# Third quarter of the up projection as seven half-size products, in a two-part encoder layer on one Trainium2 core

## The chip, the core and the metric

The kernel runs on one core of a Trainium2 chip. Five engines work beside each other, each through its own queue in order: TensorE (PE) multiplies, VectorE (DVE), ScalarE (ACT) and GpSimd (POOL) work on tiles, and SyncE (SP) issues nearly all transfers. The metric is the device time of one execution, in microseconds (us), as a median of runs.

## What is computed

One encoder layer for 512 tokens of width 1024 in float32. A token mixer (a bidirectional state-space scan and a windowed attention, merged by gates) is followed by an MLP. The change is in the MLP and in what feeds it; of the reference this matters:

```python
mixed = (g_ssd * y_ssd + g_attn * y_attn) @ w_o[l]
x = x + rmsnorm(mixed, post_mix_norm[l])
h = rmsnorm(x, pre_mlp_norm[l])
f = jnp.square(jax.nn.relu(h @ w_mlp_in[l])) @ w_mlp_out[l]   # 1024 -> 4096 -> 1024
x = x + rmsnorm(f, post_mlp_norm[l])
```

## The kernel before

**Three matmuls for one.** Each float32 operand is split into a high and a low part (`wh`, `wl` for weights, `th`, `tl` for weights split far ahead, `fh`, `fl` for activations). A product is three matmuls: high by high, high by low, low by high (`mm3`). ACT makes the high part (a cast, L1943 and L597). DVE or POOL subtracts to make the low part (L1946, and for plain weights L600 on DVE or L604 on POOL).

**Quarters.** The MLP is cut into four quarters of 1024 hidden columns. Each quarter has an up part (1024 to 1024, then squared ReLU) and a down part (1024 to 1024, summed over the quarters).

**Plain and folded.** A *plain* up product (`up_quantum`, `cm`) takes 128 hidden columns: 8 steps of 128 inputs, 3 matmuls each, so 24 matmuls of 128x512. Eight of them make a quarter: 192 matmuls. A *folded* quarter (`folded_quanta`) cuts both matrices into halves and uses seven half-size products in place of eight (Strassen's scheme in Winograd's form). Each of the seven has 2 token tiles, 4 steps and 3 matmuls, again 24 matmuls of 128x512, so a folded quarter takes 168. For that it needs sums of blocks. Of the weights: T3 = B22 - B12 (L1905), T2 = T3 + B11 (L1906), T1 = B22 - T2 (L1912), T4 = B21 - T2 (L1916), each in four tiles of 128x512. Of the activations: S1 to S4.

**What stands around a folded product.** A folded up quarter adds up its results in `up_summed` (an ACT copy at L1705 or a DVE sum at L1709), applies ReLU and square on ACT (L1712, L1714), writes halves of 16 bits apart (ACT, L1629) and stores them (`zt`). SP loads them back turned (L1638, DMA transposes). A plain product does ReLU and square on ACT (L1726, L1731) and stores `sd` (L1738). `combine` then makes the folded activations of a down quarter: on DVE four sums of 128x256 (L1784 to L1787) and four low parts (L540), on ACT four casts (L539), for each of four tiles. Down results are added into `acc` by DVE (L2049; the first into a tile is an ACT copy, L2046).

**Which quarters are folded.** `w_o`, up quarters 0 and 1 (`u0`, `u1`) and all four down quarters. Up quarters 2 and 3 are sixteen plain products. `build` lays them out by tables: two after `u1` (`LAG`), then by `STREAM` four among the products of down quarter 0, six among those of quarter 1, four among those of quarter 2, none in quarter 3.

**What sets the order.** The instructions are recorded in that order, and a `Planner` then fixes one order for each engine from costs and due times. On the chip every engine follows its list; a late operand holds up all that stands behind it. `SPL` gives three buffers each for `wh` and `wl`, so weights are split at most one and a half products ahead. Tables such as `LO_1` and `LO_2` say for each folded operand whether DVE makes the low part whole (`512`) or POOL in halves (`256`); `UPS_LO` says it for the plain products (`p` POOL, in three pieces, `d` DVE).

## Time and profile before

| | |
|---|---|
| median of 3 runs | 1026.97 us (1026.18 to 1027.3) |
| the profiled execution: its own time, its span | 1026.45 us, 1024.7 us |
| PE busy, of the span | 1016.6 us, 99% |
| DVE busy | 896.7 us, 88% |
| ACT busy | 721.1 us, 70% |
| POOL busy | 553.5 us, 54% |
| granted TensorE clock, mean | 0.999 |

Busy time overlaps between engines. Since matmuls are pipelined, the record of one (389 ns) is longer than the step from one to the next, so a run of matmuls is read by its length: 24 in 5.44 us. Stretches are given in us from the start of the span. `u0` and `u1` run from 723 to 778, down quarter 0 begins at 789, and the last matmul starts at 1017.5.

### The profile page before, as it was taken

What the parts mean: (1) busy time and instruction counts of PE and PEld (TensorE: products, weight loads), DVE (VectorE), ACT (ScalarE), POOL (GpSimd) and SP (SyncE); (2) the same over time, 40 slices, a digit from 0 to 9 for tenths busy, and PEclk for the clock granted to TensorE, in tenths of its full rate; (3) what the DMA queues carried; (4) which work ended last, traced back from release to release, by engine and by line L of the source; (5) the groups of instructions that cost most, each with busy time, mean ns of one, the idle gap of its engine ahead of it and who ended that gap; (6) DMA issues with size and microseconds to landing.
All of it is one profiled execution on the core that took longest, in us unless ns stands there. A gap on an engine that the chain in (4) does not pass through costs nothing.

```text
span 1024.7 us, 16500 instructions
## 1 busy us (share of the span) xinstructions
PE 1016.6 (99%) x5154; PEld 853.1 (83%) x5154; DVE 896.7 (88%) x1497; ACT 721.1 (70%) x1495; POOL 553.5 (54%) x571
## 2 busy tenths in 40 slices
PE   9999999999999999999999999999999999999997
PEld 8888888888888888888888888888888888888886
DVE  6886988879999899897999978789986999899997
ACT  7977959687797786968885324479999664555662
POOL 5967658476594866948898766222542223206001
PEclk9999999999999999999999999999999999999999
DMA  8389799998797999989976999875657785973482
GB/s 314 116 206 276 185 223 227 213 233 223 206 248 206 227 230 225 227 233 224 249 240 201 336 343 329 283 249 178 208 143 192 184 248 187 311 274 106 138 293 103
DMA packets 197976, 231.57 MB, mean 226 GB/s; under 512 B 102392, under 2 KB 120824, under 8 KB 197888
## 3 DMA queue, kind: packets, MB, share of 16 engines
q1 hardware_dynamic: 197600, 230.22, 79.1%
q8 instruction: 40, 0.66, 0.3%
q14 instruction: 48, 0.39, 0.1%
q10 hardware_dynamic: 288, 0.30, 0.1%
HBM read 161.97 MB, written 47.51 MB: 204 GB/s over the span
## 4 chain that ended last, share of the span: by engine, by line
PE 94%; DVE 3%; issue 1%; ACT 1%; POOL 0%; POOLq 0%; DVEq 0%
PE pp L522 58%; PE ps L522 35%; DVE wl L1946 1%; DVE tl L1946 1%; POOL wl L1946 0%; ACT wh L1943 0%; PE pp L526 0%; DVE wt L1912 0%; DVE wd L1906 0%; DVE pp L1709 0%; ACT acc L1705 0%; ACT th L1943 0%; DVE fs L1674 0%; DVE ps L1968 0%; ACT junk L2061 0%
## 5 line engine op out<-in xcount | busy, mean ns | idle before, releaser
L604 POOL TENSOR_TENSOR wl<-wr,wh 128x341 fp32r<-128x341 f32 (+1 forms) x330 | 346.2, 1064 | 267.3 <-ACT wh L597 259.6
L522 PE MATMUL pp<-h,wh 128*128 128x512 f32 x1376 | 426.3, 390 | 0.0
L522 PEld LDWEIGHTS pp<-h,wh 128*128 128x128 f32 x1376 | 256.2, 188 | 52.6 <-issue 0.7
L522 PE MATMUL pp<-h,wl 128*128 128x512 f32 x688 | 269.0, 391 | 0.0
L597 ACT CAST wh<-wr 128x1024 fp32r<-128x1024 f32 (+1 forms) x115 | 119.5, 1039 | 81.6 <-PE pp L522 48.9
L522 PEld LDWEIGHTS pp<-h,wl 128*128 128x128 f32 x688 | 129.1, 188 | 27.2 <-issue 0.5
L1943 ACT CAST wh<-wd 128x512 fp32r<-128x512 f32 x116 | 67.4, 619 | 39.6 <-PE ps L522 21.8
L1946 DVE TENSOR_TENSOR wl<-wd,wh 128x512 fp32r<-128x512 f32 x102 | 74.3, 758 | 6.6 <-ACT wh L1943 6.1
L522 PE MATMUL ps<-wl,fh 128*128 128x512 f32 x196 | 76.2, 390 | 0.3 <-POOL wl L1946 0.3
L522 PE MATMUL ps<-wh,fl 128*128 128x512 f32 x196 | 76.1, 389 | 0.0
L522 PE MATMUL ps<-wh,fh 128*128 128x512 f32 x196 | 75.4, 389 | 0.0
L1946 POOL TENSOR_TENSOR wl<-wd,wh 128x256 fp32r<-128x256 f32 x28 | 29.0, 1061 | 52.5 <-ACT wh L1943 20.9
L1326 ACT ACTIVATE n<-cb,tables 128x128 f32<-128x128 f32 x128 | 48.9, 392 | 9.3 <-DVE yT L1461 4.8
L1133 DVE SCALAR_TENSOR_TENSOR u<-pp,cv,u 128x510 f32<-128x510 f32 (+1 forms) x64 | 47.8, 747 | 6.4 <-ACT u L1129 4.2
L1946 DVE TENSOR_TENSOR tl<-wd,th 128x512 fp32r<-128x512 f32 x60 | 46.5, 799 | 5.1 <-ACT th L1943 5.0
L1327 ACT ACTIVATE m<-cb,tables 128x128 f32<-128x128 f32 x128 | 48.9, 390 | 0.0
L1322 ACT ACTIVATE rf<-rf,tables 128x128 f32<-128x128 f32 x128 | 42.1, 391 | 5.4 <-DMA rf<-csT 5.2
L522 PEld LDWEIGHTS ps<-wl,fh 128*128 128x128 f32 x196 | 36.8, 188 | 8.3 <-POOL wl L1946 0.7
L522 PEld LDWEIGHTS ps<-wh,fh 128*128 128x128 f32 x196 | 36.8, 188 | 7.7
L522 PEld LDWEIGHTS ps<-wh,fl 128*128 128x128 f32 x196 | 36.8, 188 | 7.5
L1008 DVE COPY dp<-P 128x768 uint16<-128x768 uint16 (+1 forms) x48 | 38.1, 809 | 4.6 <-ACT P L1038 3.7
L1320 POOL TENSOR_TENSOR rb<-rb,tables 128x512 f32<-128x512 f32 x32 | 39.9, 1251 | 2.7 <-DMA rb<-csT 2.6
(335 smaller groups left out, 2406.7 us busy)
## 6 DMA issues: line engine op xcount, KB each, us to landing
wr<-in_w_in_b SPq DMA_DIRECT2D x74, 512.0 KB, 5.3
wd<-in_w_mlp_out SPq DMA_DIRECT2D x76, 256.0 KB, 4.5
zt<-dp SPq DMA_DIRECT2D x56, 256.0 KB, 3.9
sd<-wd SPq DMA_DIRECT2D x48, 256.0 KB, 5.3
wd<-sd SPq DMA_DIRECT2D x48, 256.0 KB, 3.8
wd<-in_w_mlp_in SPq DMA_DIRECT2D x44, 256.0 KB, 4.9
rb<-csT SPq DMA_DIRECT2D x32, 256.0 KB, 4.6
rf<-csT SPq DMA_DIRECT2D x32, 256.0 KB, 6.1
```

The source lines that it names most:

```text
L522: self.nc.tensor.matmul(out, lhsT, rhs, start=start, stop=stop, skip_group_check=more)
L597: self.nc.scalar.copy(hi[:, :m], raw)
L604: self.nc.gpsimd.tensor_tensor(lo[:, c], raw[:, c], hi[:, c].bitcast(F32), op=ALU.subtract)
L1008: (copy or nc.vector.tensor_copy)(apart.rearrange("p (u k) -> p u k", u=2), src.bitcast(U16)[:, :2 * w].rearrange("p (k u) -> p u k", u=2))
L1133: nc.vector.scalar_tensor_tensor(u[:, a:e], ps[:, a + d:e + d], self.wtap(t, b), u[:, a:e], op0=ALU.mult, op1=ALU.add)
L1320: nc.gpsimd.tensor_tensor(v4(rb), v4(rb), cs[:, 1].unsqueeze(2).to_broadcast([128, 4, 128]), op=ALU.subtract)
L1322: nc.scalar.activation(v4(rf)[:, h], v4(rf)[:, h], AF.Identity, bias=ncs[:, 0, h:h + 1])
L1326: nc.scalar.activation(v4(n)[:, h], cb[:, 0], AF.Copy, scale=dt[:, 0, h:h + 1])
L1327: nc.scalar.activation(v4(m)[:, h], cb[:, 1], AF.Copy, scale=dt[:, 1, h:h + 1])
L1943: nc.scalar.copy(hi, src)
L1946: (nc.vector if q == 512 else nc.gpsimd).tensor_tensor(lo[:, c], src[:, c], hi[:, c].bitcast(F32), op=ALU.subtract)
```

## The change

It does these things.

- `FOLDED` is 3: the third up quarter becomes the folded `u2`. Its operands `S1` to `S4`, already made for `u0` and `u1`, are held one quarter longer. The low parts of its weights are all DVE's (`UP2_LO`).
- A string `SEQ` lays out the rest in place of `LAG`, `STREAM` and `NEXT_F`: seven products of `u2`, seven of down quarter 0, then the eight plain products that are left (`x`), six among those of down quarter 1 and two among those of quarter 2, then quarter 3. `F_AT` says when each `combine` is recorded.
- The low parts of the eight plain products are all DVE's (`UPS_LO`), in two instructions each.
- `ACCUM`: in down quarter 2, T1 and T4 are no longer DVE differences. ACT writes the negative of B11 (into a `wt` tile) and, when T2 has been split, of T2 (in place). A transfer from POOL's queue adds B12 or B21 from memory to it. That is 8 tiles.
- Smaller: halves of T1 and T4 in quarter 1 and of B22 in quarter 2 are POOL's, T2 and T3 of quarter 2 no longer. In the attention, 16 copies of 128x768 (L1008) go from DVE to ACT (`PARTED`). Scan groups 0 and 7 leave `SINGLE`, group 1 joins `JOINED`. Some lead times move by one or by a half. At the end two scalings go to ACT and POOL (`SHARED`). The planner gets costs for POOL's transfers.

In instructions (both lists counted): PE 24 matmuls of 128x512 fewer. DVE 26 low parts of folded weights (L1946), 8 weight sums (L1905, L1906), 6 sums of results (L1709) and 6 low parts of plain weights (L600) more, L1912 and L1916 the same in number. ACT 28 casts of folded weights, 8 negations, 6 copies (L1705), 8 copies of halves (L1629) more and 8 casts of plain weights fewer. POOL 33 pieces of L604 fewer, 4 halves and 8 transfers more. SP 16 transposes more.

```diff
-LO_1 = {'B11': [[(0, 256), (1, 256)], [(0, 512)]], 'B21': ...
-LO_2 = {... 'T2': [[(0, 256), (1, 256)], [(0, 512)]], ... 'T3': [[(0, 256), (1, 256)], [(0, 512)]], ...
+LO_1 = {... 'T1': [[(0, 512)], [(0, 256), (1, 256)]], ... 'T4': [[(0, 512)], [(0, 256), (1, 256)]]}
+LO_2 = {... 'B22': [[(0, 256), (1, 256)], [(0, 256), (1, 256)]], ...
-SINGLE = (0, 1, 2, 3, 4, 5, 6, 7)
+SINGLE = (1, 2, 3, 4, 5, 6)
-JOINED = (0, 3, 4, 5, 6, 7)
-FOLDED = 2
+JOINED = (0, 1, 3, 4, 5, 6, 7)
+FOLDED = 3
-SHARED = ((4, 3, 2),)
+SHARED = ((3, 2, 1), (4, 3, 1))
-PARTED = "DDD"
+PARTED = "DAD"
-UPS_LO = "pppppddppppddppdpdpp"
-STREAM = "0101011", "2110101", "2100100"
+SEQ = "uuuuuuu0000000x1x1xx111x1x12x2x22222"
+ACCUM = (2,)
+UPS_LO = "dddddddd"
...
+            if part in ACCUM and name == "T1":
+                return raw["T1", k], (("T1", k),)
+            if part in ACCUM and name == "T4":
+                return raw["B11", k], (("B11", k),) + ...
...
+                    if part in ACCUM and name in ("B11", "T2"):
+                        t = src
+                        if name == "B11":
+                            t = raw["T1", k] = get("wt")
+                        nc.scalar.activation(t, src, AF.Copy, scale=-1.0)
+                        nc.gpsimd.dma_start(t, block("B12" if name == "B11" else "B21", k), accum_op=ALU.add)
...
+        downs = {}
+        for d in SEQ + "3":
+            if d in "0123" and d not in downs:
                 for k in range(4):
-                    self.at(n() + FIRST_F[k], lambda k=k: self.up_combine(0, k))
...
+                    self.at(n() + F_AT[int(d)][k], lambda k=k, d=d: self.up_combine(int(d), k))
+                downs[d] = deque(self.folded_quanta(int(d)))
+            if d == "3":
+                self.add(*downs[d])
+            else:
+                self.add((more if d == "u" else ups if d == "x" else downs[d]).popleft())
```

On PE, at the end of `u1`, before the change (names end in buffer numbers; `h` are the normalised activations, `ps` and `pp` result banks):

```order
L522 MATMUL ps_8553<-th_9076,h_1038_8268 128x512
L522 MATMUL ps_8553<-tl_9077,h_1038_8268 128x512
L522 MATMUL ps_8553<-th_9076,h_1039_8269 128x512
L522 MATMUL pp_9230<-h_1024_8254,wh_9087 128x512
L522 MATMUL pp_9230<-h_1025_8255,wh_9087 128x512
L522 MATMUL pp_9230<-h_1024_8254,wl_9088 128x512
```

The same place after the change:

```order
L524 MATMUL ps_8559<-th_9082,h_1040_8274 128x512
L524 MATMUL ps_8559<-tl_9083,h_1040_8274 128x512
L524 MATMUL ps_8559<-th_9082,h_1041_8275 128x512
L524 MATMUL ps_9252<-wh_9095,h_1026_8260 128x512
L524 MATMUL ps_9252<-wl_9096,h_1026_8260 128x512
L524 MATMUL ps_9252<-wh_9095,h_1027_8261 128x512
```

The two plain products (first operand `h`, second `wh`) that stood between `u1` and down quarter 0 are gone from here; the first product of `u2` follows `u1` at once, and after seven such products quarter 0.

On DVE, from the last T4 sums of `u1` on, after the change (L1922 and L1923 are the sums that were L1905 and L1906, L1937 was L1916, L1967 was L1946):

```order
L1937 TENSOR_TENSOR wd_8100<-wd_8218,wd_8100 128x512
L1967 TENSOR_TENSOR tl_9070<-wd_8019,th_9069 128x512
L1967 TENSOR_TENSOR tl_9081<-wd_8098,th_9080 128x512
L1967 TENSOR_TENSOR wl_9096<-wd_9091,wh_9095 128x512
L1922 TENSOR_TENSOR wd_9193<-wd_9189,wd_9193 128x512
L1711 TENSOR_TENSOR acc_9045<-ps_8558,acc_9045 128x512
L1922 TENSOR_TENSOR wd_9195<-wd_9191,wd_9195 128x512
L1923 TENSOR_TENSOR wd_9091<-wd_9193,wd_9091 128x512
L1711 TENSOR_TENSOR acc_9059<-ps_8559,acc_9059 128x512
L1967 TENSOR_TENSOR wl_9184<-wd_9179,wh_9183 128x512
```

Low parts and sums of `u2` now fill DVE's list between the last sums of results of `u1`.

On POOL, the last part of the program, before:

```order
L604 TENSOR_TENSOR wl_10411<-wr_10400,wh_10410 128x342 x2
L604 TENSOR_TENSOR wl_10775<-wr_10723,wh_10774 128x341
L604 TENSOR_TENSOR wl_10775<-wr_10723,wh_10774 128x342 x2
L1946 TENSOR_TENSOR wl_10781<-wd_10633,wh_10780 128x256 x2
L1946 TENSOR_TENSOR wl_10824<-wd_10676,wh_10823 128x256 x2
L604 TENSOR_TENSOR wl_10864<-wr_10821,wh_10863 128x341
```

And after:

```order
L1967 TENSOR_TENSOR tl_9083<-wd_8100,th_9082 128x256 x2
L1967 TENSOR_TENSOR wl_10443<-wt_10448,wh_10442 128x256 x2
L1967 TENSOR_TENSOR wl_10508<-wt_10513,wh_10507 128x256 x2
L1967 TENSOR_TENSOR wl_10519<-wd_10050,wh_10518 128x256 x2
L1967 TENSOR_TENSOR wl_10558<-wd_10147,wh_10557 128x256 x2
L1973 DMA wt_10853<-in_w_mlp_out 128x512
L1973 DMA wt_10858<-in_w_mlp_out 128x512
L1973 DMA wt_10903<-in_w_mlp_out 128x512
L1973 DMA wt_10908<-in_w_mlp_out 128x512
L1973 DMA wd_10746<-in_w_mlp_out 128x512
L1973 DMA wd_10748<-in_w_mlp_out 128x512
```

POOL has nothing from the end of `u1` (`tl_9083`) to the halves of T1 of down quarter 1 (`wl_10443`), then two rows of T4 halves, then the transfers that add (six of the eight; two more follow the last row, and then the halves of B22 of quarter 2). The `L604` rows of before are gone.

## Rows read from the trace of the kernel before

**Rows 1.** The page: busy time by engine; the chain that ended last.

```profile
PE 1016.6 (99%) x5154; PEld 853.1 (83%) x5154; DVE 896.7 (88%) x1497; ACT 721.1 (70%) x1495; POOL 553.5 (54%) x571
PE 94%; DVE 3%; issue 1%; ACT 1%; POOL 0%; POOLq 0%; DVEq 0%
```

**Rows 2.** The waits of PE alone, 24 to 1018: total us, times, longest.

```profile
PE ps L522 <- POOL wl L1946: 0.3, 1, 0.3
```

**Rows 3.** The chain in order of time: start us, us, what.

```profile
757.72 3.11 POOL wl L1946
...
816.31 5.44 PE pp L522 x24
...
838.07 5.44 PE ps L522 x24
```

**Rows 4.** Busy us (instructions) by stretch: PE, PEld, DVE, ACT, POOL; clock, DMA share, GB/s.

```profile
720.00:760.00 40.00, 40.00 (x177) 32.91 (x176) 39.97 (x60) 37.99 (x68) 14.75 (x9) 1.00 0.55 168
760.00:778.00 18.00, 17.74 (x78) 14.36 (x78) 7.84 (x11) 17.13 (x27) 15.76 (x18) 1.00 0.70 192
778.00:854.00 76.00, 76.00 (x337) 62.90 (x336) 70.67 (x122) 53.98 (x95) 15.57 (x14) 1.00 0.76 212
854.00:940.00 86.00, 86.00 (x381) 71.22 (x380) 79.93 (x128) 44.37 (x77) 23.75 (x22) 1.00 0.69 232
940.00:1018.00 78.00, 77.74 (x355) 64.67 (x353) 71.18 (x127) 42.26 (x83) 6.97 (x8) 1.00 0.50 169
```

**Rows 5.** DVE in order of time: start us, us, instruction [idle before, releaser].

```profile
751.60 2.49 DVE L1912 TENSOR_TENSOR wt<-wd,wd 128x512 f32<-128x512 f32 x4
...
762.52 0.73 DVE L1946 TENSOR_TENSOR tl<-wd,th 128x512 fp32r<-128x512 f32 x1 [1.81 <-ACT th L1943]
...
768.29 0.70 DVE L1709 TENSOR_TENSOR pp<-pp,acc 128x512 f32<-128x512 f32 x1 [1.79 <-PE pp L522]
...
779.13 0.42 DVE L1784 TENSOR_TENSOR fs<-fT 128x256 f32<-128x256 f32 x1 [5.01 <-DMA fT<-zt]
```

**Rows 6.** Groups by shape, 670 to 1025: busy us, mean ns | idle before.

```profile
L1946 DVE TENSOR_TENSOR wl<-wd,wh 128x512 fp32r<-128x512 f32 x100 | 72.3, 754 | 6.0 <-ACT wh L1943 5.4
...
L1943 ACT CAST wh<-wd 128x512 fp32r<-128x512 f32 x113 | 65.6, 619 | 36.1 <-PE ps L522 19.1 <-PE pp L522 12.1 <-DVE wd L1916 2.5
...
L1629 ACT COPY dp<-r 128x1024 uint16<-128x1024 uint16 x16 | 16.7, 1044 | 0.3
...
L1916 DVE TENSOR_TENSOR wd<-wd,wd 128x512 f32<-128x512 f32 x16 | 12.9, 842 | 0.0
```

**Rows 7.** The line of the low parts: ns min/median/max, first and last start.

```profile
L1946 DVE TENSOR_TENSOR wl<-wd,wh x102: 676/686/1415, 649.6 to 999.8; 128x512 fp32r<-128x512 f32 x102
...
L1946 POOL TENSOR_TENSOR wl<-wd,wh x28: 735/924/3602, 649.6 to 944.2; 128x256 fp32r<-128x256 f32 x28
...
L1946 DVE TENSOR_TENSOR wl<-wt,wh x16: 680/688/693, 754.0 to 952.3; 128x512 fp32r<-128x512 f32 x16
```

**Rows 8.** POOL busy in L604 alone, by stretch.

```profile
778.00:1018.00 240.00, 32.24 (x28) 1.00 0.65 205
```

**Rows 9.** Transfers: count, KB each, median us to landing; the turned loads' issue ns.

```profile
wd<-in_w_mlp_out SPq DMA_DIRECT2D x76, 256.0 KB, 4.5
...
L1638 SPq DMA_TRANSPOSE fT<-zt x32: 1127/1246/1725, 754.4 to 834.4; - x32
```

**Rows 10.** A stretch of the scan: PE, PEld, DVE, ACT, POOL.

```profile
200.00:300.00 100.00, 100.00 (x609) 85.44 (x606) 89.11 (x158) 77.61 (x184) 67.45 (x72) 1.00 0.90 230
```

**Rows 11.** The last scalings, on DVE and on POOL.

```profile
1020.31 0.48 DVE L2080 SCALAR_TENSOR_TENSOR x<-ps,frs,x 128x256 f32<-128x256 f32 x1
...
1020.20 0.72 POOL L2077 TENSOR_TENSOR x<-x,sc 128x256 f32<-128x256 f32 x1 [0.58 <-ACT sc L2076]
```

More of the change, by code (lines that the diff above doesn't have):

```diff
@@ L41 @@
 MIX_FAR = (0,2,3,5,6,8,9,11,12)
-MIX_LEAD = (('B11', 5), ('B21', 4), ('B22', 3), ('B12', 3))
+MIX_LEAD = (('B11', 6), ('B21', 5), ('B22', 4), ('B12', 4))
 PP_BANKS = {("o", "Z"), (3, "Z"), ("u0", "Z"), ("u0", "Y"), ("u1", "Z"), ("u1", "Y")}
 PAIRS = (1, 0), (2, 3)
-SINGLE = (0, 1, 2, 3, 4, 5, 6, 7)
+SINGLE = (1, 2, 3, 4, 5, 6)
 NEXT_SCORES = False
-E_LEAD = 1
-JOINED = (0, 3, 4, 5, 6, 7)
+E_LEAD = 1.5
+JOINED = (0, 1, 3, 4, 5, 6, 7)
 ALONE = (7,)
-FOLDED = 2
+FOLDED = 3
 HALVES = 4 if FOLDED == 1 else 0
@@ L333, in duration @@
         if e == "POOL":
+            if "DMA" in kind:
+                return 1000, False
             if "pow" in str(getattr(i, "op", "")):
@@ L377, in deadlines @@
                 continue
-            c += LEAD if "DMA" in type(self.ins[n]).__name__.upper() else 0
+            c += 0 if "DMA" not in type(self.ins[n]).__name__.upper() else LEAD + SOFT + 1500 if e == "POOL" else LEAD
             late[n] = min([late[s] - self.AFTER[self.eng[s]] for s in self.post[n]] + [bound]) - c
@@ L421, in plan @@
             if e == "SP" or "DMA" in type(self.ins[n]).__name__:
-                queue = max(queue, t + ISSUE) + self.transfer(n, t)
-                free[e], end = end, queue + LAND
-                landed.append(end)
-                landed.popleft()
-                free["SP"] = max(free["SP"], min(landed) + 60)
+                soft = e == "POOL"
+                queue = max(queue, t + (ISSUE, 900)[soft]) + (1480 if soft else self.transfer(n, t))
+                free[e], end = end, queue + LAND + (0, SOFT)[soft]
+                if not soft:
+                    landed.append(end)
+                    landed.popleft()
+                    free["SP"] = max(free["SP"], min(landed) + 60)
             elif e == "PE":
@@ L1687, in flip_h2 @@
                                       "S3": [x[:, lo] for x in ft], "S4": [x[:, hi] for x in ft]}
-            self.held.setdefault(f"u{FOLDED - 1}", []).append({"S1": fs, "S3": ft})
+            self.held.setdefault(f"u{FOLDED - 1}", []).append({"S1": fs, "S3" if FOLDED < 3 else "S4": ft})
         if t2 == 0:
@@ L1885, in prepare @@
         def prepare(k):
+            if part in ACCUM:
+                a, b, c, d = (get("wd") for _ in range(4))
+                more = lambda t, src: nc.gpsimd.dma_start(t, src, accum_op=ALU.add)
+                nc.sync.dma_start(b, block("B12", k))
+                nc.sync.dma_start(c, block("B11", k))
+                nc.scalar.activation(b, b, AF.Copy, scale=-1.0)
+                more(b, block("B22", k))
+                more(c, b)
+                nc.scalar.activation(a, c, AF.Copy, scale=-1.0)
+                nc.scalar.activation(d, c, AF.Copy, scale=-1.0)
+                more(a, block("B22", k))
+                more(d, block("B21", k))
+                for t, n in ((c, "T2"), (b, "T3"), (a, "T1"), (d, "T4")):
+                    ready[n, k] = self.spill(t)
+                return
             a, b, c, d = (get("wd") for _ in range(4))
@@ L1909, in operand @@
                 return raw["B12", k], (("B12", k),)
+            if part in ACCUM and name == "T1":
+                return raw["T1", k], (("T1", k),)
+            if part in ACCUM and name == "T4":
+                return raw["B11", k], (("B11", k),) + ((("B21", k),) if order.index("A12") < order.index("A22") else ())
             if name == "T1":
@@ L2135, in build @@
         ups = deque(self.up_quantum(i) for i in range(8 * FOLDED + HALVES, 32))
[L2136 to L2156 removed]
+        downs = {}
+        for d in SEQ + "3":
+            if d in "0123" and d not in downs:
+                for k in range(4):
+                    self.at(n() + F_AT[int(d)][k], lambda k=k, d=d: self.up_combine(int(d), k))
[4 more added lines that the diff above has]
+                self.add((more if d == "u" else ups if d == "x" else downs[d]).popleft())
+        assert not more and not any(downs[d] for d in "012")
         assert not ups
```

36 lines of the change are left out of this document (7 added, 29 removed).

## The prediction

> **What bounds the kernel now.** I read the table of engines and the chain first. TensorE is busy for 1016.6 of 1024.7 us and holds 94% of the chain [rows 1]. Then the waits of PE alone: from 24 us to the last matmul there is one, of 0.3 us, on a low part that POOL makes [rows 2]; in the chain it is POOL's step at 757.72, and all else around it is PE with itself, 24 matmuls in 5.44 us or 226.7 ns each [rows 3]. The clock is 1.00 in every stretch [rows 4]. So the time falls by what PE has less to do, as long as no operand comes late. The stretches show who could be late. A row gives PE, PEld, DVE, ACT and POOL in this order: DVE is busy for 39.97 of 40 us at 720 to 760, then for 7.84 of 18, 70.67 of 76, 79.93 of 86 and 71.18 of 78; ACT is full only to 778, and from there has a quarter of its time free or more, POOL more than half [rows 4].
>
> **PE: the gain.** A plain quarter is 192 matmuls, a folded one 168, and the lists of PE for the whole program say the same: 4721 before, 4697 after. So the rival that the change doesn't take work off the bounding engine is out. At the price of rows 3 these 24 are **-5.44 us**, all on the path.
>
> **DVE: what is added, and its cover.** By the lists DVE gets from 760 on 26 low parts of folded weights, 8 weight sums, 6 sums of results and 6 low parts of plain weights more, and two scalings at the very end fewer: 44 instructions of 512 columns. A record lasts 680 to 690 ns undisturbed [rows 7], but records overlap: four L1912 take 2.49 us [rows 5], 0.62 each. 44 x 0.62 = **27.3 us**. PE also leaves 5.4 us less to do it in, so 32.7 us of idle time are wanted.
>
> The cover is DVE's idle time. From 760 to 778 it is 18 - 7.84 = 10.2 us, from 778 to 1018 it is 5.3 + 6.1 + 6.8 = 18.2 us [rows 4]: 28.4 us, 4.3 too few. A relief comes to it. POOL's pieces of plain weights, 28 of them with 32.24 us after 778 [rows 8], all go. Beside POOL a DVE instruction is slower: the same low part has a median of 688 ns from `wt`, where its spread is 680 to 693 [rows 7], and a mean of 754 from `wd` [rows 6]. The 66 ns over 100 such low parts are 6.6 us, without the sums, which are slowed too (L1916 has a mean of 842 ns, rows 6). How much of it goes with L604 is not to be seen; it lies between 0 and some 10 us, and I take **6 us**, near the one term that has rows. Then 32.7 stand against 34.4 us. The cover is just enough, with 1.7 us to spare in 250, and DVE is as full there as at 720 to 760.
>
> The Trainium skill ("SBUF — State Buffer", section "Who interferes with whom") says why such a relief should exist: a DVE instruction with two SBUF inputs contends with a GpSimd instruction that reads SBUF, since its second input comes through the shared read interface. The trace agrees: POOL's halves, 735 ns at best, reach 3602 ns [rows 7]. By the rule the relief could be as much as the whole 32 us of POOL reads that go, and the 1.05 us of the next paragraph would then be 0 and the sum 1022.0.
>
> Can a DVE that is full keep PE fed? Before, it was full from 720 to 760, and PE lost nothing till 757.7 and 18 - 17.74 = 0.26 us behind it [rows 4], so 0.26 us in some 58 us of that kind. After, the full stretch is some 235 us: 0.26 x 235 / 58 = **+1.05 us**. A part of the idle time looks hard to fill, since it ended on ACT's high part (1.81 us at 762.52), on a result of PE (1.79 us at 768.29) and on a turned load (5.01 us at 779.13) [rows 5]. But a DVE that has other rows in hand or is late itself doesn't wait for PE, and in its new list `u2`'s low parts and sums stand between the sums of `u1`'s results.
>
> **ACT.** 28 casts of folded weights and 8 negations at 0.62 us, 8 copies of halves at 1.04 [rows 6], 6 result copies (taken as casts) more, and 8 casts of plain weights at about 1 us fewer: some +26 us. After 778 ACT is idle for 22 + 42 + 36 us [rows 4], four times that. The tight place is the start: from 760 to 778 it is busy for 17.13 of 18, and its casts for `u2` begin there. A cast that is late passes its delay to DVE and from there to PE; this is in the range. **SP** gets 16 turned loads of 1.25 us at issue and 16 weight loads more and 8 stores and 16 loads fewer; the loads of 256 KB land in 4.5 us and the DMA share is 0.76 at most after 778 [rows 4, 9]. `u2`'s results are now loaded back among quarters 0 and 1 and used in quarter 2, some 100 us later. Nothing.
>
> **The scan and the tail.** There 16 copies go from DVE to ACT; in 200 to 300 DVE has 11 us free and ACT 22, and PE loses none [rows 10]. Nothing, as long as ACT takes 16 us over the whole of the scan. At the end DVE's last scaling begins at 1020.31 and POOL's at 1020.20 [rows 11]; one moved from DVE to ACT and POOL leaves the end where it is within 0.3 us.
>
> **The adding transfers.** No row shows one, or a POOL queue that issues one. From below, it is a load of 256 KB that lands in 4.5 us [rows 9], and it takes 8 sums of 0.62 us, 5 us, off DVE against the differences (which the count above has already, as L1912 and L1916 stay equal in number). From above, each issue holds POOL as long as its slowest half, 3.60 us [rows 7]. T4 is the tighter of the two: in PE's list T2's product is under way at row 4165, and T4's first matmul is row 4249, 84 x 0.2267 = 19.0 us. Negation 0.62, four issues 14.4, landing 4.5, cast 0.62, low part 0.69: 20.8 us, **1.8 us late** at the upper end, 0 at the lower. Only the two groups of four queue behind each other on POOL, then B22's halves. I am nearer to the lower end, since the half's median is 924 ns [rows 7], and take a quarter of it, **+0.45**.
>
> The Trainium skill warns of just this ("SBUF — State Buffer", section "SBUF: two separate sides"): a transfer issued from the GpSimd queue has its descriptors written by GpSimd's cores, and some DVE instructions lock these out. The page's other section, named above, infers that a tensor_tensor doesn't, since it takes the read interface alone. No row of before can show it; by the first the term would be 1.8 us and the sum 1024.4, by the second 0 and 1022.5.
>
> **The sum.** The profiled execution took 1026.45 us, 0.52 less than the median. 1026.45 - 5.44 + 1.05 + 0.45 = 1022.5; with the 0.52, **1023.0 us**.
>
> **The rivals.**
>
> *DVE takes PE's place as the bound.* If the relief is 0, DVE lacks 4.3 us. If, besides, a quarter of the 18.2 us that it was idle after 778 can't be filled, it lacks 4.5 us more. PE then waits for low parts all through `u2` and quarters 0 and 1, 8.8 us in all: 1026.97 - 5.44 + 8.8 = **1030.3 us**, slower than before. It decides from a loss of 5.44 + 2.1 = 7.5 us on. For it speaks the 70.67 of 76 us; against it that PE did not stand still beside a DVE that was wholly full. The place to fear is `u2` with quarter 0 behind it and no plain product between: some 54 rows of 0.62 us for `u2` and 44 us for quarter 0 are 77.5 us, in 76.2 us of PE's 336 matmuls. It has to live on the 10 us of before 778.
>
> *DVE is partly late.* Half of that, 4.4 us: 1026.97 - 5.44 + 4.4 = **1025.9 us**, the same as before within the bound.
>
> *The transfers are late.* T1 or T4 at the upper end, once or twice 1.8 us besides the 1.05: 1026.97 - 5.44 + 1.05 + 1.8 = **1024.4**, or up to 1026.2.
>
> *Full gain.* No loss at all: 1026.97 - 5.44 = 1021.5; the neighbour of the forecast, within its case.
>
> **How the numbers follow.** A measurement of this kernel tells some 0.2%, 2.05 us, from no change: faster is below 1024.9, slower above 1029.0. The forecast (1021.2 to 1024.4) has 0.58; DVE partly late (1024.4 to 1028) 0.18; late transfers 0.07; DVE as the bound 0.12; 0.05 is left for what I don't see, of either sign. Faster: 0.58, 0.06 of the late transfers, and 0.03 each from the edge of partly late and from the rest, about 0.68, taken as 0.67. Slower: 0.12 starts at about 1028, so two thirds of it: 0.08. Same: 0.25. The range goes from 1021.2 (the full gain and the spread of the runs) to 1026.8, where the case of partly late has been taken in to its greater part; some 0.15 lies above it and 0.03 below.
>
> **What would show it.** Right: PE's records 24 fewer in the up part, its waits after 24 us no more than 2 us in all, DVE busy for 97% or more from 770 to 940, POOL's halves nearer to 735 ns. If DVE is the bound, PE's waits stand at low parts of `u2` and quarter 0, released by L1946, with DVE at 100% ahead of them. If ACT is late, DVE's idle time ends on L1943. If transfers are late, the wait stands at T4 or T1 of quarter 2, released by a DMA. What makes the prediction wrong first is the relief: DVE's low part from `wd` staying at 754 ns beside a POOL that has little to do.

## The result and the profile after

The changed kernel takes 1030.11 us (median of 7 runs, 1029.56 to 1030.7), the kernel before beside it 1026.70 us (7 runs, 1026.18 to 1027.3). The ratio is 1.0034, with a 95% interval of 1.0022 to 1.0045: **3.4 us slower**, where the prediction said 3.9 us faster. It lies outside the range.

The profiled execution of after spans 1028.1 us, 3.4 us more than the one of before. The page's table of engines, and its chain, to hold against [rows 1]:

```profile
PE 1014.6 (99%) x5130; PEld 847.9 (82%) x5130; DVE 902.8 (88%) x1527; ACT 753.7 (73%) x1555; POOL 524.9 (51%) x552
PE 86%; DVE 4%; DMA 3%; ACT 3%; issue 1%; SPq 1%; POOL 1%; DVEq 0%; ACTq 0%; POOLq 0%
```

PE has its 24 matmuls fewer (5154 to 5130), so the 5.44 us were saved. But it holds 86% of the chain, no longer 94%: other engines and transfers now stand on it. PE's waits from 750 us on, where before had the one of [rows 2]:

```profile
PE ps L524 <- ACT fh L541: 2.1, 2, 1.3
PE ps L524 <- DVE wl L1967: 1.2, 2, 0.7
PE ps L524 <- POOL wl L1967: 1.2, 2, 1.0
PE ps L524 <- ACT acc L2073: 0.4, 1, 0.4
```

And the stretches, to hold against [rows 4] (PE, PEld, DVE, ACT, POOL; clock, DMA share, GB/s):

```profile
760.00:778.00 18.00, 16.83 (x74) 13.28 (x73) 11.29 (x17) 14.41 (x24) 12.89 (x12) 1.00 0.53 172
778.00:854.00 76.00, 75.07 (x328) 60.83 (x327) 73.03 (x130) 71.34 (x127) 0.00 (x0) 1.00 0.64 175
854.00:940.00 86.00, 85.31 (x377) 70.22 (x376) 81.20 (x141) 44.25 (x76) 13.34 (x12) 1.00 0.87 245
940.00:970.00 30.00, 27.80 (x120) 21.94 (x119) 29.58 (x57) 22.50 (x43) 6.09 (x7) 1.00 0.94 282
```

PE stands still in four places: at 764, 824 to 828, 932, and 943 to 949. ACT is as full as DVE from 778 to 854 (71.34 of 76 us; 53.98 before). From 854 on the transfers are: a DMA share of 0.87 and 0.94, where before had 0.69 and, at 940 to 970, 0.29.

**Where the time went.** To compare executions I add up, over successive matmuls, the time from start to start beyond what a matmul of that width takes without a wait (226.7 ns for 512 columns by [rows 3], and 0.42 ns less for each column fewer: steps of 320 columns have a median of 147 ns in the trace of before; less than 30 ns is left out). This is PE's *loss*, in us. It is a little more than the waits, since the step after a wait is some 0.1 us longer too, and in the scan it holds many short steps above that price, which both kernels have.

| | 0 to 24 | 24 to 600 | 600 to 755 | 755 to 778 | 778 to 850 | 850 to end |
|---|---|---|---|---|---|---|
| before | 4.3 | 27.0 | 1.8 | 0.5 | 0.0 | 0.0 |
| after | 4.7 | 28.2 | 1.8 | 1.7 | 1.9 | 4.0 |

The differences are 0.4, 1.2, 0, 1.2, 1.9 and 4.0: 8.7 us. With the gain, -5.44 + 8.7 = +3.3 us, which is the 3.4 us measured. So the question is what makes the losses of 1.9 us (at 824 to 828) and 4.0 us (at 930 to 949), and who is to blame for the rest.

### The profile page after: what moved, and what is told of

Read it like the earlier page. It is cut to its first block, busy times and chain, and to the rows that moved or that the text cites. A ratio compares the mean times of both kernels' runs of the same rounds, so it can differ in the third digit from the quotient of the medians.

```text
span 1028.1 us, 16576 instructions
## 1 busy us (share of the span) xinstructions
PE 1014.6 (99%) x5130; PEld 847.9 (82%) x5130; DVE 902.8 (88%) x1527; ACT 753.7 (73%) x1555; POOL 524.9 (51%) x552
## 4 chain that ended last, share of the span: by engine, by line
PE 86%; DVE 4%; DMA 3%; ACT 3%; issue 1%; SPq 1%; POOL 1%; DVEq 0%; ACTq 0%; POOLq 0%
PE pp L524 48%; PE ps L524 38%; DMA rb<-csT 1%; DMA E<-csE 1%; DVE u L1135 1%; DMA wd<-in_w_mlp_out 1%; DMA xt<-in_xt 0%; SPq L1885 0%; DVE w L1405 0%; DVE m L1331 0%; SPq L1306 0%; PE pp L528 0%; ACT rf L1324 0%; DVE ps L1400 0%; DVE C L1135 0%
## 5 line engine op out<-in xcount | busy, mean ns | idle before, releaser
L524 PE MATMUL pp<-h,wh 128*128 128x512 f32 x1248 | 386.8, 391 | 0.0
L606 POOL TENSOR_TENSOR wl<-wr,wh 128x342 fp32r<-128x342 f32 (+3 forms) x297 | 305.7, 1043 | 128.2 <-ACT wh L599 121.0
L524 PEld LDWEIGHTS pp<-h,wh 128*128 128x128 f32 x1248 | 232.1, 188 | 47.9 <-issue 1.0
L524 PE MATMUL pp<-h,wl 128*128 128x512 f32 x624 | 244.1, 391 | 0.0
L524 PEld LDWEIGHTS pp<-h,wl 128*128 128x128 f32 x624 | 117.2, 188 | 24.5 <-issue 0.2
L1964 ACT CAST wh<-wd 128x512 fp32r<-128x512 f32 x140 | 81.1, 619 | 29.2 <-PE ps L524 13.8
L524 PE MATMUL ps<-wl,fh 128*128 128x512 f32 x228 | 89.1, 391 | 2.4 <-DVE wl L1967 1.2
L524 PE MATMUL ps<-wh,fh 128*128 128x512 f32 x228 | 88.3, 392 | 2.5 <-ACT fh L541 2.1
L1967 DVE TENSOR_TENSOR wl<-wd,wh 128x512 fp32r<-128x512 f32 x126 | 85.3, 706 | 4.4 <-ACT wh L1964 3.3
L524 PE MATMUL ps<-wh,fl 128*128 128x512 f32 x228 | 88.6, 390 | 0.1
L1967 POOL TENSOR_TENSOR wl<-wt,wh 128x256 fp32r<-128x256 f32 x4 | 5.3, 1358 | 120.6 <-ACT wh L1964 120.6
L1967 POOL TENSOR_TENSOR wl<-wd,wh 128x256 fp32r<-128x256 f32 x28 | 29.8, 1091 | 59.0 <-ACT wh L1964 57.6
L1967 DVE TENSOR_TENSOR tl<-wd,th 128x512 fp32r<-128x512 f32 x60 | 45.8, 789 | 6.8 <-ACT th L1964 6.6
```

The lines of the kernel that those rows point to most:

```text
L524: self.nc.tensor.matmul(out, lhsT, rhs, start=start, stop=stop, skip_group_check=more)
L606: self.nc.gpsimd.tensor_tensor(lo[:, c], raw[:, c], hi[:, c].bitcast(F32), op=ALU.subtract)
L1964: nc.scalar.copy(hi, src)
L1967: (nc.vector if q == 512 else nc.gpsimd).tensor_tensor(lo[:, c], src[:, c], hi[:, c].bitcast(F32), op=ALU.subtract)
```

## The experiments

In the sets below the kernel before spread more (1025.9 to 1032.5 us), so a ratio is good to some 0.15% (1.5 us), and the losses of the profiled executions tell more than medians. All edits are to the changed kernel, whose own ratio is 1.0034. They are shown shortened: the lines that keep the planner's costs, and with them the order of its lists, as they were are left out. In runs 1 to 3, 5, 9, 13, 14, 17 and 18 the lists of all engines are in the same order as in the changed kernel (POOL's zeroing apart), so that only durations differ.

The first place is the loss at 824 to 828, the second the one at 930 to 949. Theory A, from the chain of after: queues hold up PE, ACT's at 778 to 828, then SP's and the transfers at 897 to 947. Its rival, theory B, is the prediction's: DVE alone is the bound. Three theories for the first place alone came later. B': DVE in that stretch. C: SP's turned loads ahead of quarter 0's weights. D: ACT and DVE both, each alone enough.

**Runs 1 to 3: ACT's copies, and the turned loads.**

```diff
 # part_rows, run 1
+if key[0] == "u2":
+    self.nc.gpsimd.memset(d, 0.0)
+    self.nc.scalar.copy(apart.rearrange("p (u k) -> p u k", u=2)[:, :, :32],
+                        self.halves(r).rearrange("p (k u) -> p u k", u=2)[:, :, :32])
+else:
     self.nc.scalar.copy(apart.rearrange("p (u k) -> p u k", u=2), self.halves(r).rearrange("p (k u) -> p u k", u=2))
 # turn_rows, run 2
+if key[0] in ("u2",):
+    self.nc.sync.dma_start(dst[:, at * 256:(at + 1) * 256], self.x1d[k, at][:, :256])
+    return
```

> The changed kernel, with the eight copies that set u2's 16-bit halves apart cut to 64 of 1024 columns (the rest of the tile is set to zero by POOL, which has nothing to do there); the order of every engine's list stays as it is. It leaves out most of u2's result. ACT has about 8 x 0.8 = 6.4 us less to do between 778 and 828. Theory A (queues: ACT at 778 to 828, then SP and the transfers at 897 to 947 hold up PE; DVE has enough time): the 1.9 us that PE loses at 824 to 828 go, 1028.2 us, and the 3.9 us at 930 to 948 stay. Theory B (DVE alone is the bound, the rival of the prediction): DVE's work is the same, so 1030.1 us as before within 0.4.

> The changed kernel, with u2's 16 turned loads (DMA transposes) put in their places as plain loads of the same size from another buffer; the order of every list stays. Quarter 2 gets wrong operands. Theory A: SP's queue is 16 x some 0.8 us shorter at 897 to 937 and the DMA share falls below 0.9 at 920 to 950; the 3.9 us that PE loses at 930 to 948 go for the most part: 1026.5 us (1026.0 to 1027.5), with the 1.9 us at 824 to 828 unchanged. Theory B: 1030.1 us within 0.4, since DVE does the same work.

> The two edits before together: u2's copies of halves cut to 64 columns, its 16 turned loads plain ones. Theory A: both losses go, 1024.3 us (1023.8 to 1025.5), near the 1023.0 of the prediction; what is left over it is what the start, the scan and the end of u1 lose. Theory B: 1030 us.

Run 1: 1.0033 (1.0019 to 1.0046), loss 1.9 at 778 to 850 and 4.0 behind it: nothing moved. Theory A falls for the first place. In the changed kernel the chain there (start, us, what) runs over ACT:

```profile
820.79 1.02 ACT dp L1631
...
822.28 0.61 ACT wh L1964
...
824.31 0.52 ACT wh L1964
824.83 0.52 ACT fh L541
```

With ACT relieved, in run 1, it runs over DVE:

```profile
820.36 0.65 DVE wl L1973 x2
...
822.17 0.60 DVE wd L1928
...
823.28 0.69 DVE wd L1929
...
825.52 0.60 DVE wl L1973
826.12 0.60 DVE wt L1939
```

Run 2: 0.9987 (0.9974 to 1.0001), by the ratios 4.8 us less than the changed kernel. The loss behind 850 falls from 4.0 to 1.4; the 1.9 stay. Run 3: 1.0011 (0.9995 to 1.0026), losses 2.0 and 1.7, that is run 2's with nothing from ACT's side, and 2.7 us more in the scan than run 2, with the same lists there. The 1024.3 us that theory A expected of it were missed. The turned loads of `u2` are the larger part of the second place. This is SP's list there in the changed kernel (start, us, issue):

```profile
914.66 2.54 SPq L1640 DMA_TRANSPOSE fT<-zt  x2
917.25 0.57 SPq L1083 DMA_DIRECT2D sd<-wd  x1
917.92 2.46 SPq L1640 DMA_TRANSPOSE fT<-zt  x2
920.47 1.00 SPq L1885 DMA_DIRECT2D wd<-in_w_mlp_out  x2
921.57 0.54 SPq L1740 DMA_DIRECT2D sd<-r  x1
922.16 1.63 SPq L1083 DMA_DIRECT2D sd<-wd  x3
923.89 5.96 SPq L1885 DMA_DIRECT2D wd<-in_w_mlp_out  x5
```

and in run 2, where the same loads are plain:

```profile
914.07 0.92 SPq L1641 DMA_DIRECT2D fT<-x1d  x2
916.11 0.81 SPq L1889 DMA_DIRECT2D wd<-in_w_mlp_out  x2
917.01 0.53 SPq L1744 DMA_DIRECT2D sd<-r  x1
917.58 1.80 SPq L1083 DMA_DIRECT2D sd<-wd  x3
919.48 3.37 SPq L1889 DMA_DIRECT2D wd<-in_w_mlp_out  x5
```

Two turned loads hold SP for 2.5 us, two plain ones for 0.9. The five weight loads of the next quarter are issued at 923.89 and take 5.96 us to issue, against 919.48 and 3.37. In the changed kernel the chain goes on with them (start, us, what):

```profile
925.33 1.49 SPq L1885
...
926.87 1.90 SPq L1885
...
928.86 7.50 DMA wd<-in_w_mlp_out
...
936.45 0.69 DVE wd L1922
937.14 1.21 DVE wd L1923 x2
```

A weight block lands after 7.50 us. That is not slow for this stretch: the weight loads issued from 895 to 940 land after a median of 6.4 us, against 6.6 before and 6.0 in run 2 (4.5 is the median over the whole of before, [rows 9]). It comes late because it is issued late. DVE stands idle twice (start, us, instruction, idle time and what ended it):

```profile
929.50 0.69 DVE L542 TENSOR_TENSOR fl<-fs,fh 128x512 fp32r<-128x512 f32 x1 [1.87 <-DMA sd<-wd]
936.45 0.69 DVE L1922 TENSOR_TENSOR wd<-wd,wd 128x512 f32<-128x512 f32 x1 [0.85 <-DMA wd<-in_w_mlp_out]
```

Only the second ends on a weight load. The first, ahead of PE's wait of 1.0 us at 932, ends on a store of quarter 3's sums. After them DVE's work comes in a heap.

**Run 4: without the adding transfers.**

```diff
-ACCUM = (2,)
+ACCUM = ()
```

> The changed kernel with T1 and T4 of quarter 2 as DVE differences again: 8 adding transfers (2.1 MB) and 8 ACT negations out, 8 DVE instructions of 0.62 us (5 us) in; DVE's list is in another order from there on. Theory A says that the transfers at 920 to 950 get room (the software queue took 10% of the 16 engines there), but DVE, at 29.6 of 30 us at 940 to 970, gets 5 us more: 1029 to 1032 us. If the adding transfers are the main cause of the late quarter's loss: 1026 to 1027.5 us. Theory B: 5 us of DVE work more on a DVE that bounds, 1033 to 1035 us.

1.0056 (1.0038 to 1.0074). The lists are laid out anew here. The loss at 900 to 960 falls to 1.3 us, though the turned loads are all there: the 8 transfers and their place in the queues had their part in it as well. In the changed kernel they take 31% of the 16 DMA engines from 920 to 950 (the 10% of the expectation are their share over 854 to 970; queue, packets, MB, share by the profile, whose sum can pass 100%):

```profile
q1 hardware_dynamic: 6113, 6.41, 77.2%
q0 software_dynamic: 894, 1.63, 30.7%
```

But the 5 us more of DVE work come back later, as one wait of 2.6 us before 991, ended by quarter 3's low part. DVE at 970 to 1000 is full, and the granted clock of TensorE is below 1:

```profile
970.00:1000.00 30.00, 27.38 (x114) 21.79 (x113) 29.75 (x56) 22.03 (x41) 3.97 (x5) 0.94 0.65 214
```

Behind that wait the clock stands at 0.50, the lower of its two levels (1.2 GHz, not 2.4), from 990.8 to 994.2, and steps of 0.23 us take 0.43: some 1.6 us of the 4.4 that are lost behind 960. By the ratios the adding transfers are worth about 2 us to this kernel, with intervals that overlap.

**Runs 5, 9 and 14: what holds PE at 824 to 828?**

```diff
 # operand, T2 and T3, run 5; run 14 has part in (0,)
+if part == "u2":
+    a, b, c = (x[:, :63] for x in (a, b, c))
 tt(b, a, b, op=ALU.subtract)
 tt(c, b, c, op=ALU.add)
 # operand, T4
+n = 63 if part == "u2" else 512
+tt(t[:, :n], raw["B21", k][:, :n], t[:, :n], op=ALU.subtract)
 # turn_rows, run 9: as run 2, with
+if key[0] in ("u0", "u1", "u2"):
```

> The changed kernel, with 12 of u2's 16 weight sums on DVE (T3, T2 and T4, in place) cut to 63 of 512 columns; the order of every list stays. u2 gets wrong weights. DVE has about 12 x 0.47 = 5.6 us less to do between 755 and 815; ACT has the same. Theory B' (at 815 to 835 DVE is the bound: with ACT relieved the chain there ran over DVE's low parts and sums): the 1.9 us lost there go to 0.6 or less, the 1.2 us at the end of u1 may shrink a little, the 4.0 us at 900 to 960 stay. Theory ACT: the loss at 815 to 835 stays at 1.5 to 1.9. In the median 1.3 to 2 us less than the changed kernel by the first, the same by the second.

> The changed kernel, with all 48 turned loads of the three folded up quarters put in their places as plain loads of the same size from another buffer; the order of every list stays. Quarters 0 to 2 get wrong operands. Theory C (SP's queue: the turned loads, 1.25 us of issue each, stand ahead of the weight loads of the next quarter, at 798 to 818 as at 897 to 937, so that DVE and ACT get their work in a heap; this is why neither a shorter ACT nor a shorter DVE moved the loss at 815 to 835): that loss goes from 1.9 us to 0.6 or less, and the one at 900 to 960 to 1.4 or less as with u2's loads alone; some 4 to 4.5 us less than the changed kernel. Theory D (ACT and DVE are both full there, each alone enough): the 1.9 us stay.

> The changed kernel with 12 of quarter 0's 16 weight sums cut to 63 columns, those that stand in DVE's list at 815 to 835; the same order, wrong weights for quarter 0. DVE has 5.6 us less to do in that stretch itself, ACT the same. If DVE's heap there is what holds PE: 1.9 us go to 0.6 or less. By theory D ACT alone still holds it: 1 to 1.9 us.

Run 5: 1.0034 (1.002 to 1.0048), loss 1.9 at the first place, but 5.4 at the second, where 4.0 were expected. There a wait of 2.1 us comes at 934, and behind it the clock is granted at 0.50 from 935.9 to 939.3, so that the stretch has a mean of 0.94 (as above: stretch, engines, clock, DMA share, GB/s):

```profile
930.00:960.00 30.00, 26.83 (x110) 21.00 (x109) 27.26 (x50) 17.40 (x31) 3.95 (x5) 0.94 1.02 249
```

That is some 1.6 us; without it run 5 has 3.8 there. Run 9: 0.9992 (0.9978 to 1.0006), losses 1.9 and 1.4, as in run 2. Run 14: 1.0033 (1.0021 to 1.0045), loss 1.8. None of the three, each alone, moves the first place; theories B' and C fall there. In the changed kernel and the six runs with its lists that relieve at most one of the two engines (1, 2, 3, 5, 9 and 14) the loss there is 1.8 to 2.0, so it repeats well from execution to execution. The stretch of run 14 has DVE idle for 2.6 of 13 us and PE no better, with ACT full:

```profile
818.00:831.00 13.00, 12.06 (x51) 9.04 (x50) 10.44 (x25) 12.85 (x23) 0.00 (x0) 1.00 0.74 249
```

while run 1's has ACT idle for 3.2 us and DVE full:

```profile
818.00:831.00 13.00, 11.78 (x50) 8.90 (x49) 12.97 (x23) 9.78 (x21) 0.00 (x0) 1.00 0.69 244
```

**Runs 13, 17 and 18: several at once.** Run 13 is run 1, run 5 and run 14 together, run 17 is run 13 and run 2, run 18 cuts sums of quarters 1 and 2 as well.

```diff
+if part in ("u2", 0):            # runs 13 and 17
+if part in ("u2", 0, 1, 2):      # run 18
+    a, b, c = (x[:, :63] for x in (a, b, c))
```

> The changed kernel with ACT and DVE both relieved, in the same order of every list: u2's eight copies of halves cut to 64 columns (ACT, 6.4 us less at 778 to 828), and 12 of 16 weight sums of u2 and 12 of quarter 0 cut to 63 columns (DVE, 5.6 us less ahead of 815 and 5.6 us less behind it). u2 and quarter 0 get wrong operands. Theory D (both engines are full at 815 to 830, and each alone is enough to hold PE): the 1.9 us there go to 0.6 or less. If they stay, it is neither engine's load but the order, or a buffer that comes free too late.

> Run 13 (ACT and DVE relieved around 815 to 835) and u2's turned loads as plain ones, all at once, in the same order of every list; wrong operands in u2 and quarters 0 and 2. If the two losses are separate and have these causes, they go together: 0.6 us or less at 815 to 835 and 1.5 or less at 900 to 960, 3.8 us less loss of PE than in the changed kernel from 755 on.

> As the run before, and 12 of quarter 1's and 8 of quarter 2's weight sums cut to 63 columns too: DVE has 9 us less at 830 to 950. If what is left at 944 (1.2 us, ended by ACT's fh, whose source is a DVE sum) is a DVE that is full, it goes: 0.3 us or less at 900 to 960. If it is the order, it stays at 1.2 to 1.5.

Run 13: 1.0042 (1.0028 to 1.0055), and the loss at 778 to 850 falls to 0.6 us, for the first time. That is theory D: ACT and DVE both hold PE there, and each alone is enough. It rests on the losses of profiled executions alone; no ratio shows it (run 13 is no faster than run 1, run 17 no faster than run 2). Runs 5 and 14 together, with ACT as it was, were not run; against DVE alone stands run 14, where DVE had 2.6 us idle in the stretch itself. Run 17: 0.9992 (0.9969 to 1.0014), losses 1.4 and 1.4; run 18: 0.9982 (0.9968 to 0.9997), 1.1 and 0.9. The second place adds up as expected in run 17; the first is short of its mark (0.6) in both, and run 18's second place is short of its own (0.3). The chain of run 17 names what comes next at the first place, and ACT's waits at 818 to 832 agree:

```profile
825.24 4.83 DMA zt<-dp
...
830.15 0.59 ACT acc L2088
...
830.79 2.33 PE ps L526 x9
```

```profile
ACT acc L2088 <- DMA zt<-dp: 1.3, 1, 1.3
```

The first tile of quarter 0's sums takes a place in the pool that a store of `u2`'s halves gives back when it has landed. Behind the two engines stands a pool that is full; that was read from the chain, not tried. The last 1.2 us at 944 to 948 are partly DVE: 0.65 us are left of them in run 18.

The medians agree on the turned loads. The ratios of runs 2, 3, 9 and 17, with plain loads, have a mean of 0.9996; those of the changed kernel and runs 1, 5, 13 and 14, without, of 1.0035. The 0.4% between them is 4.1 us, more than the 2.3 to 2.9 us of loss. Some of the rest is clock: the executions have a mean granted clock of 0.9982 with plain loads and 0.9974 without, which by an estimate (0.0008 of 1028 us) is 0.8 us. The profiled execution of the changed kernel has no stretch at the lower level from 5 us to its last matmul.

**Run 6: the turned loads from ACT's queue.**

```diff
-self.nc.sync.dma_start_transpose(
+(self.nc.scalar if key[0] == "u2" else self.nc.sync).dma_start_transpose(
```

> The changed kernel, with u2's 16 turned loads issued from ACT's queue in place of SP's; the result is the reference's. If SP's queue is the limit (16 x 1.25 us of issue ahead of the weight loads of quarters 2 and 3), the weights come earlier and the loss at 900 to 960 falls from 4.0 to 1 to 2 us, if ACT's waits for a free tile don't hold up its casts. If the transfers themselves are the limit (the DMA share of 1.2 at 930 to 940), it stays at 3 to 4 us, since they move the same data in the same way.

1.0119 (1.0104 to 1.0134); the loss behind 850 is 14.5 us, a part of it in two stretches of 3.4 us at a granted clock of 0.50, from 920.0 and 933.7. SP is free of them, but now ACT's casts stand behind turned loads that wait and land late (chain, start, us, what):

```profile
903.80 4.05 DMA fT<-zt
907.87 9.86 DMA fT<-zt
...
919.17 2.73 DMA fT<-zt
...
924.97 6.92 DMA fT<-zt
```

Theory A's 1 to 2 us and its rival's 3 to 4 were both missed. It tells neither for the queue nor for the transfers alone: both are in that chain.

**Runs 7, 8, 10, 11, 15 and 16: attempts at a better version.**

```diff
-SEQ = "uuuuuuu0000000x1x1xx111x1x12x2x22222"
+SEQ = "uuuuuuu00x000x001x11x11x1x12x2x22222"      # run 7
+SEQ = "uuuuuuux00000001x1xx111x1x12x2x22222"      # runs 15, 16
-F_AT = ((-2.0, -2.5, -1.5, -1.5), (-3, -2.5, -2, -2), (-3, -3, -2, -2), (-4.5, -4.5, -5.0, -3.5))
+F_AT = ((-2.0, -2.5, -1.5, -1.5), (-3, -2.5, -2, -2), (-4, -4, -3, -3), (-4.5, -4.5, -5.0, -3.5))      # run 16
 # run 8: second entry of T1, T4, B22, B21 in UP2_LO and of T2, B11 in LO_0
-[(0, 512)]
+[(0, 256), (1, 256)]
 # runs 10, 11, in prepare; the stores of spill likewise
-nc.sync.dma_start(t, block(n, k))
+(nc.gpsimd if part == 3 else nc.sync).dma_start(t, block(n, k))
 # run 11, in load
-nc.sync.dma_start(raw[name, k], ready.get((name, k), None) if name[0] == "T" else block(name, k))
+(nc.gpsimd if part in (0,) else nc.sync).dma_start(raw[name, k], ready.get((name, k), None) if name[0] == "T" else block(name, k))
```

> The changed kernel, with two of the eight plain products moved forward among the products of quarter 0 and one of the others a place forward; the result is the reference's. A plain product gives PE 5.44 us for some 1.3 us of DVE and 2.2 us of ACT, so quarter 0 gets room: by the theory that DVE and ACT are too full at 778 to 828 the 1.9 us lost there shrink (the first of the two stands behind the loss's place, so to 1 to 1.9), but quarter 1 loses that room, and its transfers crowd more: the loss at 900 to 960 stays or grows (4 to 6 us). 1029.5 to 1032 us.

> The changed kernel, with 12 low parts (8 of u2's weights, 4 of quarter 0's) made by POOL in halves, where POOL has nothing to do; the result is the reference's. DVE has 12 x 0.6 = 7.4 us less at 778 to 835. If DVE's own work is the limit there, the 1.9 us go; if POOL's reads slow DVE as much as they take off it (24 halves of some 1 us), they stay. A late half would show as a new wait on POOL's low part, 1 us or so each. 1028.2 us by the first, 1030 to 1031 by the second; the 4.0 us at 900 to 960 stay.

> The changed kernel, with the 16 block loads and 16 spill stores that make quarter 3's weight sums ahead of time issued from POOL's queue in place of SP's (POOL has little to do at 778 to 917); the result is the reference's. SP gets some 17 us of issue less at 850 to 925. Theory C: the weight loads of quarter 2 come earlier and the loss at 900 to 960 falls from 4.0 to 1 to 2 us, the one at 815 to 835 stays: 1027.5 to 1028.5 us. If the transfer engines and not the queue are the limit: 3 to 5 us there, no gain, 1030 us or more.

> As the run before, and the 16 weight loads of down quarter 0 from POOL's queue too; the result is the reference's. Theory C: these loads no longer stand behind the turned loads of quarters 0 and 1, so the loss at 815 to 835 falls to 0.6 or less as well, and the kernel takes 1025.5 to 1027 us, no slower than before the change. If POOL's transfers land too late, the wait moves to a weight sum or a cast of quarter 0 behind a transfer, and it gets slower than the run before.

> The changed kernel with the first of the eight plain products moved from behind quarter 0 to ahead of it, between u2 and quarter 0; the result is the reference's. PE gets 5.44 us of work there for 1.3 us of DVE and 2.2 us of ACT, as the two plain products gave it before the change. If the heap of work at 815 to 835 is the cause, the loss there goes to 0.6 or less, whatever engine it is; quarter 1 then follows quarter 0 at once, and may lose 0 to 2 us at 855 to 870. The 4.0 us at 900 to 960 stay. 1028 to 1030 us.

> As the run before, and quarter 2's activations are made one product earlier (u2's turned loads begin some 5 us sooner); the result is the reference's. If the loss at 900 to 960 is that SP's queue has u2's turned loads ahead of the weights of quarter 2, spreading them wider takes 1 to 2.5 us of the 4.0 away: 1026 to 1028 us. If the transfers' whole amount at 854 to 970 is the limit, it stays at 3.5 to 4.5.

| run | ratio (95%) | loss 778 to 850 | loss 850 to end |
|---|---|---|---|
| 7, two plain products in quarter 0 | 1.0070 (1.0044 to 1.0095) | 4.2 | 6.8 |
| 8, 12 low parts on POOL | 1.0088 (1.0067 to 1.0109) | 4.7 | 5.4 |
| 10, sums ahead of time on POOL's queue | 1.0184 (1.0168 to 1.0199) | 2.0 | 21.9 |
| 11, quarter 0's loads too | 1.0187 (1.0148 to 1.0225) | 15.4 | 4.3 |
| 15, a plain product ahead of quarter 0 | 1.0120 (1.0080 to 1.0159) | 3.0 | 8.6 |
| 16, and quarter 2's activations earlier | 1.0139 (1.0120 to 1.0159) | 3.1 | 12.9 |

None beats either kernel, and the gains that were expected of runs 10, 11, 15 and 16 did not come. All six made the planner lay out the lists anew, so they tell less of causes than the others. Except in run 8, part of the loss is clock: each of these traces has one to three stretches of 3.4 or 6.8 us in the MLP at a granted clock of 0.50, at 827.9 and 947.4 in run 7. Run 8 shows the price of the halves: POOL's halves from `wd` have a median of 1177 ns against 951 in the changed kernel, and the loss at 778 to 850 rises from 1.9 to 4.7 though DVE has 7.4 us less to do. In run 10 PE's wait of 5.9 us from about 908 ends on ACT's cast, and the chain to it goes over the sums of quarter 3 that DVE makes ahead of time. In runs 15 and 16 the scan, whose lists are those of the changed kernel, lost 36.0 and 32.0 us; a part of their slowness is not the edit's. Why a plain product ahead of quarter 0 doesn't help, as two of them did before, was not settled.

**Run 12: the scan as before.**

```diff
-PARTED = "DAD"
+PARTED = "DDD"      # and SINGLE, JOINED, E_LEAD, MIX_LEAD, LAST, HEADS as before
```

> The changed kernel with the tables of the scan and the attention as before (copies of L1008 on DVE, SINGLE, JOINED and the lead times); the MLP as changed. The result is the reference's. PE's loss at 24 to 600 was 28.2 us after the change and 27.0 before, in one execution each. If the moved copies cost something: 27.0 to 27.5 us there, and 0.7 to 1.2 us less in all. If that is only the spread of executions: 27 to 30 us, the same time within 0.6 us. The losses at 755 to 960 stay by either.

1.0027 (1.0016 to 1.0038), loss at 24 to 600 29.1 us. With the changed kernel's lists for the scan, the other runs of these sets had 28.6 to 36.0 there. So the 1.2 us between 27.0 and 28.2 can't be told from the spread of executions, and what the scan's share is stays open.

## Why the prediction was wrong, step by step

- **The bound and the gain** were right: 24 matmuls, 5.44 us, and PE is what the time is counted on (the profile counts 5154 and 5130 matmuls where the lists say 4721 and 4697; the difference is the same).
- **SP: "Nothing."** This step failed, and it is the larger part. I held 16 issues of 1.25 us and 8 stores against a mean DMA share. But a queue is served in order: 16 turned loads, 21.3 us of issue, are put between the weight loads of quarters 2 and 3 at 897 to 937, where SP before had none of them (its last turned load was at 834.4, [rows 9]) and issued weights ten in a row (7.33 us from 906.72). Measured: 2.3 to 2.9 us of loss (run 2, 3 and 9 against the changed kernel, run 17 against run 13), 4.1 by the ratios. They do it together with the adding transfers: without those, run 4 loses 1.3 us there with the turned loads in place. The share of 0.76 at most that I quoted was before's; it became 0.87 and 0.94. Whether SP's time or the transfers' is the tighter was not settled, since run 2 cuts both; that the weight loads land no later after their issue than before, in the median, speaks for SP's order, but an issue itself took up to 1.90 us there (0.96 before, 1.11 in run 2).
- **ACT: "+26 us ... four times that".** The sum was right (23.2 us more from 760 to 1018 or 1021), the comparison wrong: 100 us of idle time, of which 78 lie behind 854, don't hide work that comes at 778 to 829. There ACT is busy for 49.99 of 51 us, fuller than DVE (48.32). I had named the start as the tight place and put it "in the range" without a price. The price is 1.9 us, together with DVE; by the losses of runs 1, 14 and 13 either engine is enough.
- **DVE: the cover and the relief.** DVE's busy time from 760 to the last matmul rose from 229.6 to 244.8 us, by 15.2 and not by 27.3 - 6 = 21.3: at the prediction's own price the relief was 12 us, twice what I took. The low part from `wd` now has a mean of 702 ns over 124, where [rows 6] has 754. By what the Trainium skill says ("SBUF — State Buffer", section "Who interferes with whom") less reading by POOL should speed up DVE, and the trace agrees, with 12 us against the 32 us of POOL's work in L604 that went. So the first thing that I expected to fail held. Two of the signs of being right failed: DVE is busy for 159.60 of 170 us from 770 to 940, 94% and not 97%, and POOL's halves from `wd` are no shorter (a median of 951 ns over the trace, 924 in [rows 7]).
- **The step behind it failed:** "0.26 us in some 58 us of that kind" was an average over 58 us of which only the first 40 were of that kind: DVE had 10 of the last 18 us free. What happened at 818 to 831 or behind late weights was not in it. That both engines are full is not enough to tell: from 720 to 760 before, ACT was busy for 37.99 of 40 us beside DVE's 39.97 [rows 4], and PE lost nothing. What the two stretches differ in was not tried; the full one before has 40 us, the one of after had run for 46 us from 778 when PE first waited.
- **The rival "DVE takes PE's place as the bound"** gives 1030.3 us, and 1030.1 were measured. That is chance. Its mechanism, low parts late all through `u2` and quarters 0 and 1 for lack of relief, did not happen: `u2` itself and the time from 830 to 930 lose nothing. What it had right is the place, `u2` with quarter 0 behind it and no plain product between, though the 44 us of its sum for quarter 0 stand on no row.
- **The adding transfers.** PE waited for none of them directly. POOL holds 0.87 to 1.21 us for an issue (my upper end was 3.60), and they land after 5.8 to 9.3 us (I took 4.5). By the ratios of run 4 they give about 2 us more than they cost, though they crowd the second place. The Trainium skill's warning ("SBUF — State Buffer", section "SBUF: two separate sides") of DVE instructions that keep GpSimd from writing descriptors can't be seen here: DVE works with no gap above 0.13 us from 921.8 to 927.5, and the four issues there take about 1 us each all the same.
- **The end of `u1`** loses 1.2 us more, which I had not looked at. POOL's last halves are late. They do not wait for ACT's casts: POOL works on eight of them without idle time between. These are rows of after (start, us, instruction; then ns min/median/max of POOL's first four halves):

```profile
759.11 10.54 POOL L1967 TENSOR_TENSOR wl<-wd,wh 128x256 fp32r<-128x256 f32 x8 [20.43 <-ACT wh L1964]
L1967 POOL TENSOR_TENSOR wl<-wd,wh x4: 721/730/4332, 759.1 to 764.8; 128x256 fp32r<-128x256 f32 x4
761.57 1.28 DVE L1937 TENSOR_TENSOR wd<-wd,wd 128x512 f32<-128x512 f32 x2
```

  And of before, where POOL's longest half, the first of these, took 3602 ns [rows 7]:

```profile
757.71 9.83 POOL L1946 TENSOR_TENSOR wl<-wd,wh 128x256 fp32r<-128x256 f32 x8 [20.43 <-DVE tl L1946]
760.02 0.69 DVE L1916 TENSOR_TENSOR wd<-wd,wd 128x512 f32<-128x512 f32 x1
```

  POOL starts at the same point of PE's work (PE is 1.4 us later by then). Its first half ends 0.6 us after DVE's last row in both, at 763.44 and 761.31, and DVE's row of work is longer by one instruction: 0.7 us, as much as the half. PE's first wait there is longer by that much. The other 0.5 us are a second wait: in PE's new list four matmuls of that product, and not one, stand ahead of 22 of another product. This is read from the rows, not tried, and it varies: in run 2, with the same lists, the first half took 2.53 us beside DVE instructions of 1.2 us, and the loss from 755 to 778 was 1.25 and not 1.7.
- **The scan and the start** lose 1.6 us more in the profiled pair, where I had "nothing". Run 12 can't tell it from the spread, and the cause stays open.
- **Two small sums** are off and change nothing: 1026.97 - 5.44 + 1.05 is 1022.6 and not 1022.5, and 0.58, 0.06 and twice 0.03 make 0.70 and not 0.68.

In the sum: predicted -5.44 + 1.05 + 0.45, measured -5.44 + 4.0 (of it 2.3 or more from the turned loads, beside the adding transfers; the rest in part a late heap on DVE) + 1.9 + 1.2 + 1.6.
